# Sparse-attention indexer: three of eight heads summed on GpSimd, five on VectorE out of PSUM

## The chip, the cores and the metric

The kernel runs on one core of a Trainium2 chip. The metric is the device time of one execution in microseconds. The profile is of one execution, taken by the hardware profiler on the same core. The engines are TensorE (PE; PEld is its weight load), VectorE (DVE), ScalarE (ACT), GpSimd (POOL) and SyncE (SP, which issues DMAs).

## What is computed

Two layers of an encoder over 16 learned meta tokens and 1024 frames, width 1024. Layer 0 mixes tokens with chunked gated linear attention, layer 1 with sparse attention; a SwiGLU block follows each. The change lies in layer 1. Per block of 128 queries:

```python
s_idx = einsum('bqhd,bsd->bqhs', q_idx, k_idx) * IDX_DIM ** -0.5     # 8 indexer heads of 64
score = einsum('bqhs,bqh->bqs', relu(s_idx), w_idx)                  # weighted sum over heads
score = where(admissible, score, -inf)                               # chunk-causal
top_val, top_idx = top_k(score, 256)
logits = q_lat . c[top_idx] * ATT_HEAD_DIM ** -0.5 + rel_bias        # attention over the 256 keys
```

The kernel doesn't gather. It finds the 256th largest score of every query by bisection over the bits of the scores, writes a mask that is 0 for chosen keys and -1e30 elsewhere, and attends densely. Among equal scores the earlier keys win, as in `top_k`.

## The kernel before

Every f32 product is made of three passes over a high and a low part in fp32r (`mm3`, L223 to L227; `split`, L219 to L221, makes the parts: the high one on ScalarE, the low one on VectorE or on the engine named). All matmul results go through eight PSUM tiles of 512 columns (`ps`, L179). The program is written in one order; the compiler issues each engine's instructions in about that order and moves some ahead where they are ready. `Later` (L60) holds closures that fall due after a number of `tick` calls, one per unit of work.

Layer 1's mixer is `dsa` (L857). Its stages:

- **Keys and queries of the indexer** (L876 to L896). `kxh` and `kxl` hold the keys' parts, `wt` the head weights, which are turned into `wx`, one column per block and head. `index_queries` makes the queries' parts `qx`, in two ranges of frames and for two heads at a time.
- **Scores** (`score`, L898 to L915). A block b has 144 + 128 b keys, cut in pieces of at most 512 columns (one piece for blocks 1 and 2, two each for 3 to 6, three for 7; block 0 needs none). Per block, head and piece: two matmuls into PSUM, a Relu on ScalarE from PSUM into one of three `rt` buffers (L907), and on VectorE a multiply by the head's weight into `sc` (head 0, L910) or a multiply-add onto `sc` (L912). The early blocks 1 to 3 are interleaved with the second range of queries, two heads at a time; then the late blocks 4 to 7 follow, heads 0 to 7 of one block after the other. The `kx` and `relu` pools are closed behind it, and their space is used again by the masks and the top-k.
- **Top-k beside projections** (L937 to L982). A list of units (the latent `c`, L990 to L1031; the query projections, L1033 to L1055; `parts`, which splits the queries of heads 0 to 5 into `xh` and `xl`; keys and values of the first head pair) is issued in order, and steps of `topk` (L1057) are taken between them by a list of costs: 66 steps of bisection and 8 for masks. Blocks are in two groups. A step counts on ScalarE (L1090) and VectorE (L1093) how many scores lie above a candidate; `decide` (L1095) makes the next candidate on GpSimd (L1102 to L1106), in a fixed order, so it waits in GpSimd's queue behind whatever was issued there. Counting of the next step needs it.
- The latent units hold their results in PSUM until three of them are there; then VectorE scales them (L1018) and a closure, due 3 to 5 ticks later, transposes each on TensorE (`turn`, L1022, L1026) and splits it.
- `parts` handles three frame ranges, each in two groups j of three heads. For j = 1 (named in `QPOOL`) it splits head by head with GpSimd making the low parts, for j = 0 in one piece of 1032 columns with VectorE.
- **Masks** (L1189 to L1202). Per block: ScalarE takes the sign of threshold minus score (`sg`, and its sum), VectorE tests it for zero (L1196), makes a running count of the equal ones (`pre`, L1197), computes how many equal ones are still needed (L1198, L1199), and forms the mask (L1200, L1201).
- **Attention** (L1246): GpSimd adds the relative bias to the mask (L1263), then logits, softmax and mixing, pair by pair of blocks.

Weights that were split beforehand come by DMAs queued on GpSimd (`load_parts`, L195): the latent's at `w.ahead()` (L932), those of dq0 when the latent's are taken (L1001).

## Time and profile before

| | us |
|---|---|
| three runs | 2604.9, 2607.8, 2607.78 (median 2607.78) |
| the profiled execution | 2605.77 |
| its span in the profile | 2604.0 |
| mean granted clock of TensorE | 0.982 of full speed |

The page gives totals per engine, the span in 40 slices, DMA queues, the chain that ended last and the costliest groups. A busy TensorE there is not TensorE at its peak, since matmuls are pipelined; a row of a merged timeline gives its start, the time to the end of its last instruction, and how many. Layer 1's mixer runs from about 1285 to 1745 us of the span; the rows further down are from there.

### The profile page before, as it was taken

Reading aid. Unit: us, or ns where it says so; the run is one execution under the profiler, and the core shown is the slowest. Engines: PE = TensorE matmul, PEld = TensorE weight load, DVE = VectorE, ACT = ScalarE, POOL = GpSimd, SP = SyncE. Lnnn points to the kernel's source line nnn. Section 1 sums busy time; section 2 is a strip of 40 time slices with the busy share of each in tenths; the row PEclk is TensorE's granted clock in tenths of the full one; section 3 lists DMA queues with packets and bytes.
Section 4 is the critical chain, followed back from the end, with each engine's and each line's share of the span. In section 5 each row is a group of like instructions: output and inputs, shape, how many; then the busy total and the mean of one; then the engine's idle time right before and its main releaser. Section 6 shows DMA issues by size and latency. Waiting matters only on the chain.

```text
span 2604.0 us, 37955 instructions
## 1 busy us (share of the span) xinstructions
PE 2513.8 (97%) x15072; PEld 2333.6 (90%) x15072; DVE 1358.0 (52%) x2915; ACT 952.7 (37%) x1970; POOL 382.0 (15%) x582
## 2 busy tenths in 40 slices
PE   6999999999999999999898969999999999999997
PEld 6899999999999999999878959999988888888887
DVE  7565566643333333444679997762633333333336
ACT  5664453521111111112568867761511111111114
POOL 3000000111111111110203455440200000000001
PEclk9999999999999999999899969999999999999999
DMA  3103013123333333331311101122011111111111
GB/s 119 41 27 116 25 49 105 43 86 122 121 102 120 116 117 112 116 118 66 117 65 51 64 25 42 64 96 85 33 65 49 49 49 49 47 42 42 49 49 65
DMA packets 68788, 190.00 MB, mean 73 GB/s; under 512 B 7065, under 2 KB 18609, under 8 KB 65794
## 3 DMA queue, kind: packets, MB, share of 16 engines
q1 hardware_dynamic: 62642, 154.31, 17.6%
q0 software_dynamic: 5968, 33.26, 3.7%
q8 instruction: 118, 1.93, 0.3%
q14 instruction: 60, 0.49, 0.1%
HBM read 150.74 MB, written 41.58 MB: 74 GB/s over the span
## 4 chain that ended last, share of the span: by engine, by line
PE 41%; DVE 4%; issue 2%; ACT 2%; POOL 1%; DMA 0%; ACTq 0%; DVEq 0%; POOLq 0%
PE ps L226 13%; PE ps L227 13%; PE ps L225 13%; PE ps L1310 1%; DVE jd L1093 1%; POOL xl L221 1%; DVE sc L912 1%; PE ps L1322 1%; PE ps L903 0%; DVE pre L1197 0%; ACT ja L1090 0%; ACT rt L907 0%; PE ps L1298 0%; PE ps L905 0%; DVE h L332 0%
## 5 line engine op out<-in xcount | busy, mean ns | idle before, releaser
L225 PE MATMUL ps<-xh,wh 128*128 128x344 f32 (+6 forms) x2808 | 947.7, 338 | 5.8 <-ACT wh L191 4.1
L226 PE MATMUL ps<-xl,wh 128*128 128x344 f32 (+6 forms) x2808 | 943.9, 336 | 0.8 <-POOL xl L221 0.6
L227 PE MATMUL ps<-xh,wl 128*128 128x344 f32 (+6 forms) x2808 | 941.4, 335 | 3.0 <-DVE wl L192 3.0
L225 PEld LDWEIGHTS ps<-xh,wh 128*128 128x128 f32 x2808 | 530.3, 189 | 37.1 <-ACT wh L191 4.4
L226 PEld LDWEIGHTS ps<-xl,wh 128*128 128x128 f32 x2808 | 530.7, 189 | 30.2 <-POOL xl L221 1.4
L227 PEld LDWEIGHTS ps<-xh,wl 128*128 128x128 f32 x2808 | 530.3, 189 | 30.1 <-DVE wl L192 3.3
L703 DVE TENSOR_TENSOR t<-sg,ps 128x344 f32<-128x344 f32 (+4 forms) x116 | 65.1, 561 | 643.8 <-PE ps L227 643.0
L191 ACT CAST wh<-wraw 128x1056 fp32r<-128x1056 f32 (+2 forms) x160 | 163.9, 1049 | 582.4 <-PE ps L226 570.8
L716 DVE TENSOR_TENSOR h<-h,ps 128x344 f32<-128x344 f32 (+3 forms) x456 | 250.8, 566 | 163.6 <-PE ps L227 163.5
L225 PE MATMUL ps<-hh,wh 128*128 128x512 f32 (+2 forms) x800 | 280.3, 350 | 0.0
L226 PE MATMUL ps<-hl,wh 128*128 128x512 f32 (+2 forms) x800 | 280.0, 350 | 0.0
L227 PE MATMUL ps<-hh,wl 128*128 128x512 f32 (+2 forms) x800 | 279.8, 350 | 0.0
L192 DVE TENSOR_TENSOR wl<-wraw,wh 128x1056 fp32r<-128x1056 f32 (+2 forms) x158 | 195.1, 1257 | 73.8 <-ACT wh L191 72.9
L225 PE MATMUL ps<-wh,xh 128*128 128x256 f32 (+9 forms) x560 | 173.5, 310 | 11.5 <-ACT xh L220 7.4
L227 PE MATMUL ps<-wh,xl 128*128 128x256 f32 (+9 forms) x560 | 167.9, 300 | 4.1 <-POOL xl L221 2.1
L702 ACT ACTIVATE sg<-ps 128x344 f32<-128x344 f32 (+4 forms) x116 | 57.8, 498 | 303.5 <-PE ps L227 299.0
L226 PE MATMUL ps<-wl,xh 128*128 128x256 f32 (+9 forms) x560 | 166.8, 298 | 0.0
L220 ACT CAST hh<-t 128x344 fp32r<-128x344 f32 (+4 forms) x116 | 60.0, 517 | 285.3 <-DVE t L703 285.3
L225 PEld LDWEIGHTS ps<-hh,wh 128*128 128x128 f32 x800 | 150.1, 188 | 14.6
L226 PEld LDWEIGHTS ps<-hl,wh 128*128 128x128 f32 x800 | 150.3, 188 | 14.3
L227 PEld LDWEIGHTS ps<-hh,wl 128*128 128x128 f32 x800 | 150.5, 188 | 13.9
L225 PEld LDWEIGHTS ps<-wh,xh 128*128 128x128 f32 x560 | 109.6, 196 | 17.7 <-ACT xh L220 8.1
(286 smaller groups left out, 3378.6 us busy)
## 6 DMA issues: line engine op xcount, KB each, us to landing
wraw<-in_w_fi SPq DMA_DIRECT2D x44, 528.0 KB, 3.8
wraw<-in_w_fi SPq DMA_DIRECT2D x44, 496.0 KB, 4.9
wraw<-in_w_fo SPq DMA_DIRECT2D x22, 528.0 KB, 3.8
wraw<-in_w_fo SPq DMA_DIRECT2D x22, 496.0 KB, 5.1
s_skew<-s_rel POOLq DMA_DIRECT2D x8, 583.5 KB, 13.0
h<-in_ht SPq DMA_DIRECT2D x8, 520.0 KB, 5.8
wraw<-s_skew SPq DMA_DIRECT2D x8, 520.0 KB, 3.5
sg<-in_w_dq SPq DMA_DIRECT2D x16, 256.0 KB, 4.3
```

Source lines behind the costliest of these rows:

```text
L191: nc.scalar.copy(hi[:, a:e], r[:, : e - a])
L192: self.wlow.tensor_sub(lo[:, a:e], r[:, : e - a], hi[:, a:e].bitcast(F32))
L220: self.nc.scalar.copy(hi, src)
L221: (low or self.nc.vector).tensor_sub(lo, src, hi.bitcast(F32))
L225: mm(p, sh, mh, start=first, stop=False, skip_group_check=True)
L226: mm(p, sh, ml, start=False, stop=False, skip_group_check=True)
L227: mm(p, sl, mh, start=False, stop=last, skip_group_check=True)
L702: nc.scalar.activation(sg[:, :n], pg[:, :n], AF.Silu)
L703: v.tensor_mul(t[:, :n], sg[:, :n], pu[:, :n])
L716: v.tensor_add(self.h[:, d, a : a + n], self.h[:, d, a : a + n], p[:, :n])
L912: eng.scalar_tensor_tensor(o, rt, wx[:, b, hd : hd + 1], o, op0=OP.mult, op1=OP.add)
L1093: v.tensor_scalar(j[:, :n], mu(b), cand, None, op0=OP.is_lt, op1=OP.add, accum_out=out)
```

## The change

- `EARLY_HEADS = 3`: for heads 0 to 2 ScalarE's Relu still writes `rt` (four buffers now), but GpSimd does the sum: a multiply by the weight into `sc` for head 0, a multiply in place and an addition onto `sc` for heads 1 and 2. For heads 3 to 7 the Relu is written in place in PSUM and VectorE multiplies and adds from there onto `sc`.
- The late blocks are issued in another order: heads 0 to 2 of block 4, heads 0 to 2 of block 5, heads 3 to 7 of block 4, heads 0 to 2 of block 6, heads 3 to 7 of block 5, and so on; block 7's heads 3 to 7 come last. `w.ahead()` stands at the same place of the program.
- `QPOOL = (0, 1)`: the low parts of the queries of heads 0 to 5 are all made on GpSimd, head by head; their high parts are six casts per frame range where there were one wide and three.
- The transposes of the latent are due 5 to 7 ticks later instead of 3 to 5.
- Masks: the equality test is left out; ScalarE squares the sign, so that 0 marks an equal key, and the running count subtracts a tile of ones from it. The counts are negative now, and signs and the comparison in L1198 to L1200 turn accordingly. One memset of `ones` (1040 bf16 columns) is new.

```diff
+EARLY_HEADS = 3
-QPOOL, KEYS0, PC = (1,), 0, 1.0
+QPOOL, KEYS0, PC = (0, 1), 0, 1.0
...
-            with tc.tile_pool(name="kx", bufs=1) as kp, tc.tile_pool(name="relu", bufs=3) as rp:
+            with tc.tile_pool(name="kx", bufs=1) as kp, tc.tile_pool(name="relu", bufs=4) as rp:
...
                         nc.tensor.matmul(p, qx[:, hd, t], kxl[:, s0 : s0 + n], start=False, stop=True)
+                        o, wt = sc[:, off[b] + s0 : off[b] + s0 + n], wx[:, b, hd : hd + 1]
+                        if hd >= EARLY_HEADS:
+                            nc.scalar.activation(p, p, AF.Relu)
+                            v.scalar_tensor_tensor(o, p, wt, o, op0=OP.mult, op1=OP.add)
+                            continue
+
                         rt = rp.tile([128, 512], F32, name="rt")[:, :n]
                         nc.scalar.activation(rt, p, AF.Relu)
-                        o = sc[:, off[b] + s0 : off[b] + s0 + n]
                         if hd == 0:
-                            eng.tensor_scalar_mul(o, rt, wx[:, b, hd : hd + 1])
+                            nc.gpsimd.tensor_scalar_mul(o, rt, wt)
                         else:
-                            eng.scalar_tensor_tensor(o, rt, wx[:, b, hd : hd + 1], o,
-                                                     op0=OP.mult, op1=OP.add)
+                            nc.gpsimd.tensor_scalar_mul(rt, rt, wt)
+                            nc.gpsimd.tensor_add(o, o, rt)
...
-                w.ahead()
-                for b in range(4, 8):
-                    for hd in range(8):
-                        score(b, hd)
+                    if e == 3:
+                        w.ahead()
+
+                late = [[(b, hd) for hd in range(EARLY_HEADS, 8)] for b in range(4, 8)]
+                first = [[(b, hd) for hd in range(EARLY_HEADS)] for b in range(4, 8)] + [[]]
+                for b, hd in first[0] + sum((x + y for x, y in zip(first[1:], late)), []):
+                    score(b, hd)
...
-                self.later.at(3 + i % 3, lambda i=i, c=c: turn(i, c))
+                self.later.at(5 + i % 3, lambda i=i, c=c: turn(i, c))
...
+        ones = pool.tile([128, T], BF16, name="ones")
+        v.memset(ones, 1.0)
...
-            eq = mk(b)
+            other = mk(b)
...
-            v.tensor_scalar(eq, sg, 0.0, None, op0=OP.is_equal)
-            v.tensor_tensor_scan(pre, eq, eq, 0.0, op0=OP.add, op1=OP.bypass)
-            v.tensor_scalar(need, bal, 0.5, TOPK - n / 2, op0=OP.mult, op1=OP.add)
+            nc.scalar.activation(other, sg, AF.Square)
+
+            v.tensor_tensor_scan(pre, other, ones[:, :n], 0.0, op0=OP.add, op1=OP.subtract)
+            v.tensor_scalar(need, bal, -0.5, n / 2 - TOPK, op0=OP.mult, op1=OP.add)
             v.scalar_tensor_tensor(need, pre[:, n - 1 : n], 0.5, need, op0=OP.mult, op1=OP.add)
-            v.scalar_tensor_tensor(sg, pre, need, sg, op0=OP.is_le, op1=OP.subtract)
+            v.scalar_tensor_tensor(sg, pre, need, sg, op0=OP.is_ge, op1=OP.subtract)
```

## Rows read from the trace of the kernel before

**Rows 1.** The page's first part: busy time, share of the span, instructions of each engine.

```profile
PE 2513.8 (97%) x15072; PEld 2333.6 (90%) x15072; DVE 1358.0 (52%) x2915; ACT 952.7 (37%) x1970; POOL 382.0 (15%) x582
```

**Rows 2.** Busy time in five stretches (us; busy, instructions per engine; granted clock, DMA).

```profile
core 0: us, PE busy (x) PEld busy (x) DVE busy (x) ACT busy (x) POOL busy (x), PEclk, DMA share, GB/s
1336.80:1374.50 37.70, 37.53 (x171) 24.11 (x172) 37.67 (x82) 34.52 (x75) 0.00 (x0) 1.00 0.07 29
1374.50:1391.00 16.50, 9.06 (x78) 8.88 (x77) 13.44 (x68) 12.94 (x26) 3.31 (x11) 0.85 0.19 65
1391.00:1495.00 104.00, 104.00 (x679) 103.90 (x680) 102.15 (x271) 87.86 (x208) 48.97 (x210) 0.97 0.17 62
1495.00:1515.00 20.00, 9.06 (x49) 8.33 (x47) 17.39 (x45) 14.06 (x33) 14.48 (x39) 0.77 0.01 2
1515.00:1548.00 33.00, 20.76 (x83) 18.06 (x83) 32.94 (x77) 17.14 (x45) 11.68 (x11) 0.60 0.09 32
```

**Rows 3.** Timeline of the late scores, VectorE and ScalarE (start us, busy us, instructions merged).

```profile
1364.07 10.39 DVE L912 SCALAR_TENSOR_TENSOR sc<-rt,wx,sc 128x352 f32<-128x352 f32 x21
...
1336.76 35.82 ACT L907 ACTIVATE rt<-ps 128x264 f32<-128x264 f32 x72 [0.15 <-DVE sc L915]
```

**Rows 4.** Instructions that write xl, 1370 to 1560 us (duration ns min/median/max).

```profile
L221 POOL TENSOR_TENSOR xl<-qf,xh x9: 897/944/1946, 1495.9 to 1519.3; 128x344 fp32r<-128x344 f32 x6, 128x336 fp32r<-128x336 f32 x3
L1052 DVE SCALAR_TENSOR_TENSOR xl<-ps,xh x6: 498/506/511, 1492.5 to 1514.9; 128x344 fp32r<-128x344 f32 x4, 128x336 fp32r<-128x336 f32 x2
L221 DVE TENSOR_TENSOR xl<-qf,xh x3: 1200/1264/1852, 1497.5 to 1516.5; 128x1032 fp32r<-128x1032 f32 x2, 128x1008 fp32r<-128x1008 f32 x1
```

**Rows 5.** Waits, 1270 to 1400 us and 1391 to 1500 us (us in total, times, longest).

```profile
PE ps L1026 <- DVE qf L1018: 7.4, 1, 7.4
...
ACT qf L1043 <- PE ps L227: 2.8, 2, 2.1
```

**Rows 6.** Groups by shape, GpSimd, whole run (busy us, mean ns of one).

```profile
L213 POOL CAST eh<-sg 128x512 fp32r<-128x512 f32 x54 | 35.4, 656 | 526.1 <-DMA sg<-in_w_dq 156.1 <-DMA sg<-in_w_do 155.3 <-DMA sg<-in_w_qidx 92.3
L221 POOL TENSOR_TENSOR xl<-gkv,xh 128x256 fp32r<-128x256 f32 x32 | 23.6, 739 | 23.6 <-ACT xh L220 23.6
L1106 POOL TENSOR_SCALAR flip<-cand 128x4 f32<-128x4 f32 x29 | 6.7, 231 | 2.5
L360 POOL TENSOR_SCALAR w<-mean 96x128 fp32r<-96x128 f32 x4 | 2.0, 545 | 0.0
```

**Rows 7.** Timeline of GpSimd, 1332 us and 1495 to 1521 us (start us, busy us).

```profile
1332.51 0.53 POOL L200 DMA_DIRECT2D wh<-s_dq_h  x1 [14.60 <-PE ps L227]
...
1495.87 3.71 POOL L221 TENSOR_TENSOR xl<-qf,xh 128x344 fp32r<-128x344 f32 x3
...
1516.60 3.77 POOL L221 TENSOR_TENSOR xl<-qf,xh 128x336 fp32r<-128x336 f32 x3 [2.50 <-ACT xh L220]
```

**Rows 8.** Timeline of VectorE, 1382 us and 1500 to 1530 us (in brackets: idle before, releaser).

```profile
1382.26 0.12 DVE L1186 MEMSET mask<- 128x72 uint32 x1
...
1500.40 0.90 DVE L1093 TENSOR_SCALAR_CACHE_REDUCE jd<-mask,cand 128x656 bf16<-128x656 uint16 x1 [1.61 <-POOL cand L1104]
...
1517.63 0.86 DVE L1129 TENSOR_SCALAR y<-x 128x3 f32<-128x3 f32 x1
...
1527.56 0.32 DVE L1196 TENSOR_SCALAR mask<-sg 128x656 bf16<-128x656 bf16 x1
...
1527.89 1.26 DVE L1196 TENSOR_SCALAR mask<-sg 128x784 bf16<-128x784 bf16 x1
```

**Rows 9.** Groups by shape, ScalarE, whole run (busy us, mean ns of one).

```profile
L1090 ACT ACTIVATE ja<-mask,cand 128x1040 bf16<-128x1040 uint16 x31 | 36.0, 1161 | 7.8 <-POOL cand L1104 6.5 <-DVE mask L1168 0.7
...
L1090 ACT ACTIVATE ja<-mask,cand 128x272 bf16<-128x272 uint16 x31 | 15.8, 509 | 0.0
```

**Rows 10.** DMA issues, 1300 to 1500 us (KB each, median us to landing).

```profile
wh<-s_dq_h POOLq DMA_DIRECT2D x4, 1024.0 KB, 5.4
```

**Rows 11.** Instructions that read wh, 1375 to 1420 us (first and last start).

```profile
L225 PEld LDWEIGHTS ps<-xh,wh x29: 187/188/191, 1405.8 to 1419.6; 128*128 128x128 f32 x29
```

More of the change, by code (lines that the diff above doesn't have):

```diff
@@ L871, in dsa @@
             sc = dp.tile([128, off[8]], F32, name="sc")
-            with tc.tile_pool(name="kx", bufs=1) as kp, tc.tile_pool(name="relu", bufs=3) as rp:
+            with tc.tile_pool(name="kx", bufs=1) as kp, tc.tile_pool(name="relu", bufs=4) as rp:
                 kxh = kp.tile([128, T], F32R, name="kxh")
                 kxl = kp.tile([128, T], F32R, name="kxl")
-                wt = kp.tile([128, T], F32, name="wt")
+                hw = kp.tile([128, T], F32, name="wt")
                 for a, n in ALL:
@@ L880, in dsa @@
                         nc.scalar.copy(kxh[r : r + 64, s], p[0:64, :n])
-                    nc.scalar.copy(wt[64:128, s], p[64:128, :n])
+                    nc.scalar.copy(hw[64:128, s], p[64:128, :n])
                     for r in (0, 64):
@@ L899, in score @@
                     t = slice((b - 1) * 128, b * 128)
-                    eng = v
                     for s0, n in cut(nkeys(b)):
@@ L922, in dsa @@
                             a = META + 128 * b
-                            nc.tensor.transpose(p[:, b * 64 : b * 64 + 64], wt[64:128, a : a + 128],
+                            nc.tensor.transpose(p[:, b * 64 : b * 64 + 64], hw[64:128, a : a + 128],
                                                 self.ident[64:128, 64:128])
```

## The prediction, made before the changed kernel was run

> **What bounds the kernel now.** I read the page's totals first: TensorE is busy for 97% of the span [rows 1], so a change to the other engines can only act where TensorE idles or is paced. Then busy time by stretch [rows 2], which finds that place, the indexer and its top-k. In 1336.8 to 1374.5 (scores of blocks 4 to 7) VectorE has 37.67 of 37.70 us in use and GpSimd does nothing. In 1391 to 1495 (bisection beside the query projections) VectorE has 102.15 of 104 us, in 1515 to 1548 (masks) 32.94 of 33. TensorE's matmul rows also fill 1391 to 1495, but it idles for 7.4 us before that, for 10.9 us in 1495 to 1515 and 12.2 us in 1515 to 1548. TensorE therefore has slack, and VectorE's queue sets when attention starts: what delays or shortens it moves the end nearly one for one.
>
> Third, the timeline of the late scores [rows 3]. ScalarE issues 72 Relus in 35.82 us, 0.50 us apart. The last 21 VectorE sums take 10.39 us, also 0.495 us each, and end at 1374.5. Relu follows sum because only three rt buffers stand between them. Until 1374.5 no bisection starts. Last, the waits [rows 5]: the 7.4 us of TensorE before 1391 is one wait, L1026 (transposes of the latent) for VectorE's L1018; ScalarE twice waits for a query projection, 2.8 us in all.
>
> **The change, part by part.** I sum against the profiled execution (2605.8 us, span 2604.0); it lies 2.0 us under the median of the three runs, and I take nothing for that.
>
> *Scores, VectorE and ScalarE.* Of 104 VectorE sums 39 go, 27 of them late (9 key pieces x 3 heads). The 45 late ones that remain read PSUM instead of rt. The nearest row that reads PSUM, L1052, takes 0.506 us at 344 columns [rows 4], so I keep 0.495 us: 45 x 0.495 = 22.3 us. VectorE gets slack. ScalarE keeps its Relus, now 45 of the 72 in place; if it can't go faster than 0.50 us apart it ends at 1372.6, so the gain here is at most about 2 us. In-place tiles hold their PSUM bank until VectorE has read; with 8 banks I charge nothing.
>
> *Scores, GpSimd.* Late, three heads need 27 multiplies and 18 additions, of 391 columns on average (3520 columns per head in 9 pieces). An addition: GpSimd's subtraction of two f32 tiles takes 0.944 us at 344 columns [rows 4] and 0.739 at 256 [rows 6], so 1.05 us at 391; 18 x 1.05 = 19.0 us. For a multiply no row has this width. Its own kind, TENSOR_SCALAR, takes 0.231 us at 4 columns and 0.545 at 128 [rows 6]. Drawn on in a straight line (2.53 ns a column) that makes 0.545 + 263 x 0.00253 = 1.21 us; with the steepest slope that the CAST row allows (0.656 us / 512 = 1.28 ns) 0.88 us; and if the multiply were a CAST altogether, 0.656 x 391 / 512 = 0.50 us. The row nearest in kind is TENSOR_SCALAR, so I take the middle of the first two, 1.05 us: 28.4 us (23.8 to 32.7; as a CAST 13.5). GpSimd's late work is then 47.4 us (42.8 to 51.7; 32.5).
>
> GpSimd can't begin it before the first late Relu at 1336.8, since the early blocks' pieces come first in the program. It ends at 1384.2. Block 7 comes last in the new order, and VectorE's five heads add onto GpSimd's three: behind GpSimd's last piece stand 5 sums (2.5 us, if the heads of a piece go together) to 13 (6.4 us, in the order written). The trace has Relus issued between casts that the program lists first, so order bends to readiness: 2.5 us, end 1386.7. Against 1374.5 that is **+12.2 us** (1382.1 to 1394.9: +7.6 to +20.4). The fourth rt buffer lets ScalarE run one piece further ahead and doesn't make GpSimd faster.
>
> The dq0 load queued on GpSimd moves behind this work: issued at 1332.5 [rows 7], it would go at 1384. It lands 5.4 us later [rows 10], and its first use, 1405.8 [rows 11], moves back too, so nothing.
>
> *Latent transposes two units later.* More projection work stands ahead of L1026, so its 7.4 us of idle TensorE is filled. That pays only where VectorE or ScalarE waits for TensorE later: the 2.8 us [rows 5]. I take **-1** (-2.8 to 0).
>
> *Low parts of queries.* Three VectorE subtractions go, 1.2 to 1.85 us each [rows 4], and GpSimd gets nine more in three bunches; the old bunches take 3.71 and 3.77 us, first and last of three [rows 7]. Behind the first two stand the decisions (L1102 to L1106), on which the next counts on VectorE and ScalarE wait. In the first, VectorE already idles 1.61 us for a decision [rows 8] after its own subtraction, so removing that frees nothing; three more ahead of a decision cost up to 3.7 us. Two places at 0 to 3.7: I take half, +3.7. The third bunch meets the mask code. There a TENSOR_SCALAR of 3 columns, L1129, takes 0.86 us on VectorE [rows 8] beside GpSimd's subtractions, some 0.7 more than its size explains; three more subtractions, 3 x 0.7 = 2.1, less the freed 1.2, give +0.9. Sum **+4.6** (-1.2 to +8.3).
>
> The Trainium skill (SBUF — State Buffer, Who interferes with whom) says that such VectorE instructions and GpSimd share a port pair that one of them holds for its whole instruction. The trace agrees in kind (0.86 us). Held for three whole subtractions, VectorE would lose 3.7 instead of 2.1 us, and the sum would be 1.6 us higher.
>
> *Masks.* Seven is_equal tests leave VectorE: 0.32 us at 656 columns, but 1.26 at 784, beside a GpSimd addition [rows 8]: 7 x 0.32 + 0.9 = 3.1 us. If the hold merely passes to the next instruction, 2.2. A memset of ones comes: 72 words take 0.12 us [rows 8], 520 words up to 0.87; I take 0.4. Seven squares come to ScalarE, 0.51 to 1.16 us by the bisection's rows at 272 and 1040 columns [rows 9]; ScalarE is busy for 17.14 of 33 us there [rows 2] and two sg buffers let it run ahead, so only the first, 0.5 us, is exposed. Bound: VectorE waits for a square once per pair of blocks, 4 x 0.84 = 3.4. The scan has the same width and I leave its price. The other sum's low end takes ones and the first square at nothing (-3.1). Sum -3.1 + 0.4 + 0.2 = **-2.5** (-3.1 to +1.6), the first square half covered by a query cast.
>
> 12.2 - 1 + 4.6 - 2.5 = +13.3: 2605.8 + 13.3 = 2619.1, **2619 us**.
>
> **Rivals.** *GpSimd multiplies cheaply, faster.* For: its CAST, one input like the multiply, takes 0.656 us for 512 columns. Against: TENSOR_SCALAR takes nearly that for 128. At 0.50 us the late work ends at 1336.8 + 32.5 = 1369.3 and VectorE's tail at 1371.8, with ScalarE's end at 1372.6: -2. With fast GpSimd the decisions aren't late (-1.2), transposes -1, masks -3.1: 2605.8 - 7.3 = 2598.5 us. Its point is where GpSimd's work is 35.2 us, a multiply of (35.2 - 19.0) / 27 = 0.60 us; below it the score stage shortens. The Trainium skill (GPSIMD Engine Reference, 4.1 Engine selection) calls one-input work on GpSimd roughly line-rate, which speaks for this rival; no row here shows it for TENSOR_SCALAR. Chance 0.22.
>
> *Costs and savings cancel, no change.* Multiply at the lower slope (+7.6), decisions find gaps (-1.2), transposes pay in full (-2.8), masks -2.7: +0.9, 2606.7 us. For: VectorE's new idle time can take other blocks' sign counts, and the compiler may move late multiplies forward into GpSimd's earlier gap. Chance 0.20.
>
> *The forecast, a late GpSimd.* 0.58. Own range 2610 to 2632; all upper bounds together would be +30.3, 2636.
>
> **How the numbers follow.** A measurement of this kernel can tell about 0.2%, 5.2 us, from no change: 2602.6 to 2613.0. The three cases fall faster, same, slower: 0.22, 0.20, 0.58. The range runs from 2597, which takes in most of the cheap rival, to 2632.
>
> **What would show it.** GpSimd nearly full from 1337 to about 1384, multiplies near 1.05 us, VectorE with idle time released by GpSimd in the scores, and the first sign count (L1136, now at 1375) 10 us later. Decisions behind six subtractions, with VectorE idle 3 to 5 us twice. No is_equal on VectorE, and TensorE's wait at L1026 gone. Multiplies at or under 0.6 us, or a first sign count by 1373, would make it wrong, as would attention starting on time in spite of late scores.

## The result, and the profile after

| | before | after |
|---|---|---|
| median | 2607.79 us (2604.9 to 2608.03, 4 runs) | 2635.44 us (2634.08 to 2637.3, 4 runs) |
| profiled execution, span | 2605.77, 2604.0 | 2634.08, 2632.3 |

The changed kernel is slower, ratio 1.011 with a 95% interval of 1.0095 to 1.0125: 27.7 us, where the forecast said 13 and its range ended at 2632. The sign and the place were right, the size was off by a factor of two. Of the runs further down, one execution of e10 took 13901 us and is left out of its median.

To see where the time went, four points are marked in both traces: ScalarE's first wide cast of queries, VectorE's first sign count (start of the bisection), the cast of the last decision for the first group of blocks (the four with 128x4; the other group's follows 1.8 us later in both kernels), and the first 128x128 transposes of the attention. First the timelines of the kernel before at these points.

```profile
1309.00 0.58 ACT L895 CAST qx<-ps 64x512 fp32r<-64x512 f32 x1 [3.08 <-PE ps L227]
...
1375.07 1.23 DVE L1136 TENSOR_SCALAR_CACHE_REDUCE jd<-sc 128x1040 bf16<-128x1040 uint16 x1
...
1513.73 0.17 DVE L1155 CAST th<-cand 128x4 uint16<-128x4 f32 x1
...
1548.26 0.90 PE L1310 MATMUL ps<-ident,sc 128*128 128x128 f32 x3 [1.51 <-DVE mask L1202]
```

The same four points after:

```profile
1307.07 0.58 ACT L896 CAST qx<-ps 64x512 fp32r<-64x512 f32 x1 [3.08 <-PE ps L228]
...
1398.08 1.23 DVE L1144 TENSOR_SCALAR_CACHE_REDUCE jd<-sc 128x1040 bf16<-128x1040 uint16 x1
...
1540.59 0.17 DVE L1163 CAST th<-cand 128x4 uint16<-128x4 f32 x1
...
1576.16 0.90 PE L1321 MATMUL ps<-ident,sc 128*128 128x128 f32 x3 [1.61 <-DVE sm L1289]
```

The differences give three stretches, used from here on: **scores** 66.07 us before and 91.01 after (+24.9), **bisection** 138.66 and 142.51 (+3.9), **masks** 34.53 and 35.57 (+1.0). The first point itself lies anywhere from 1307 to 1312 us in the runs, whatever the kernel.

Busy time after, which answers to [rows 1]:

```profile
PE 2519.2 (96%) x15072; PEld 2342.3 (89%) x15072; DVE 1341.8 (51%) x2867; ACT 954.6 (36%) x1983; POOL 455.2 (17%) x656
```

Two stretches, the early blocks and the late scores; the second answers to the first of [rows 2]:

```profile
core 0: us, PE busy (x) PEld busy (x) DVE busy (x) ACT busy (x) POOL busy (x), PEclk, DMA share, GB/s
1307.00:1341.20 34.20, 30.47 (x143) 24.38 (x141) 13.38 (x25) 16.00 (x42) 20.73 (x24) 0.95 0.27 92
1341.20:1397.50 56.30, 43.12 (x168) 34.83 (x168) 25.90 (x56) 30.73 (x73) 50.79 (x47) 0.76 0.08 27
```

VectorE's total fell by 16.2 us against [rows 1] and GpSimd's rose by 73.2. In the late scores VectorE now works 25.90 of 56.30 us and GpSimd 50.79: the bound seems to have passed to GpSimd, which e3 tests. TensorE, which had work in 37.53 of 37.70 us there before, idles 13 of 56; its granted clock is 0.76 in the mean there, between its two levels of 1.2 and 2.4 GHz, and was 1.00. The timeline of GpSimd (start, busy, instructions merged):

```profile
1308.11 0.98 POOL L915 TENSOR_SCALAR sc<-rt,wx 128x272 f32<-128x272 f32 x1 [21.49 <-ACT rt L913]
...
1325.93 1.43 POOL L918 TENSOR_TENSOR sc<-sc,rt 128x264 f32<-128x264 f32 x2
...
1341.40 2.19 POOL L915 TENSOR_SCALAR sc<-rt,wx 128x328 f32<-128x328 f32 x2 [3.27 <-ACT rt L913]
1343.58 2.18 POOL L917 TENSOR_SCALAR rt<-rt,wx 128x328 f32<-128x328 f32 x2
1345.73 1.70 POOL L918 TENSOR_TENSOR sc<-sc,rt 128x328 f32<-128x328 f32 x2
...
1353.75 2.50 POOL L917 TENSOR_SCALAR rt<-rt,wx 128x392 f32<-128x392 f32 x2
1356.22 2.00 POOL L918 TENSOR_TENSOR sc<-sc,rt 128x392 f32<-128x392 f32 x2
...
1389.23 1.80 POOL L918 TENSOR_TENSOR sc<-sc,rt 128x352 f32<-128x352 f32 x2
```

Two blocks of work without gaps: the early blocks' sums from 1308.1 to 1327.4, and the late ones from 1341.40 to 1391.03, which is 49.6 us. A multiply (TENSOR_SCALAR) of 392 columns takes 1.25 us, an addition 1.00. VectorE's timeline shows who waits:

```profile
1323.15 0.50 DVE L909 SCALAR_TENSOR_TENSOR sc<-ps,wx,sc 128x272 f32<-128x272 f32 x1 [5.00 <-POOL sc L918]
...
1350.47 0.56 DVE L909 SCALAR_TENSOR_TENSOR sc<-ps,wx,sc 128x328 f32<-128x328 f32 x1 [7.34 <-POOL sc L918]
...
1384.02 6.58 DVE L909 SCALAR_TENSOR_TENSOR sc<-ps,wx,sc 128x456 f32<-128x456 f32 x11 [11.87 <-ACT ps L908]
...
1390.60 6.87 DVE L909 SCALAR_TENSOR_TENSOR sc<-ps,wx,sc 128x352 f32<-128x352 f32 x14
```

Behind GpSimd's end at 1391.03 stand 13 sums, until 1397.47 (one of the 14 in the last row starts before it). The wait of 11.87 us ends with a Relu on ScalarE, not with GpSimd. ScalarE's Relus into rt wait 21.3 us in this stretch for GpSimd's sums, which free the buffers; e3 asks whether four buffers are the bound. In the early blocks head 3's sum waits for GpSimd (5.00 us). The next query parts stand behind it in VectorE's queue, and the second cast of the third pair of heads, on ScalarE, waits for them:

```profile
1328.64 0.58 ACT L896 CAST qx<-ps 64x512 fp32r<-64x512 f32 x1 [4.37 <-DVE qx L897]
```

### The profile page after: what moved, and what is told of

Same layout as the page of the kernel before. It is cut to its first block, busy times and chain, and to the rows that moved or that the text cites. A ratio compares the mean times of both kernels' runs of the same rounds, so it can differ in the third digit from the quotient of the medians.

```text
span 2632.3 us, 37984 instructions
## 1 busy us (share of the span) xinstructions
PE 2519.2 (96%) x15072; PEld 2342.3 (89%) x15072; DVE 1341.8 (51%) x2867; ACT 954.6 (36%) x1983; POOL 455.2 (17%) x656
## 4 chain that ended last, share of the span: by engine, by line
PE 42%; DVE 3%; POOL 3%; issue 1%; ACT 1%; DMA 0%; ACTq 0%; DVEq 0%; POOLq 0%
PE ps L227 13%; PE ps L228 13%; PE ps L226 13%; PE ps L1321 1%; POOL rt L917 1%; POOL sc L918 1%; POOL xl L222 1%; POOL sc L915 1%; PE ps L1333 1%; DVE pre L1208 0%; DVE jd L1101 0%; PE ps L1309 0%; DVE h L333 0%; DVE sg L1211 0%; ACT L321 0%
## 5 line engine op out<-in xcount | busy, mean ns | idle before, releaser
L227 PEld LDWEIGHTS ps<-xl,wh 128*128 128x128 f32 x2808 | 531.4, 189 | 30.4 <-POOL xl L222 1.4
L294 POOL TENSOR_TENSOR nb<-nb,nq 128x256 f32<-128x256 f32 x12 | 9.1, 758 | 711.7 <-ACT nq L292 711.7
```

The costliest lines, as they stand in the source:

```text
L227: mm(p, sh, ml, start=False, stop=False, skip_group_check=True)
```

## The experiments

Every run was timed beside the kernel before on the same chip, whose medians were 2605.85 (e1 to e4), 2605.53 (e5, e6, e7, e10), 2605.81 (e8, e9, e11, e12) and 2604.48 us (e13 to e16). Differences in the text are between medians; the ratio is worked out from the runs together and differs from that of the medians by up to 0.04%. The last three columns are the stretches of one profiled execution, read off as above. In the ten kernels, the one before among them, whose low parts and transposes are unchanged, the bisection took 138.56 to 139.26 us, so differences under 0.7 us in that column say nothing.

| run | median us | ratio, 95% interval | scores | bisection | masks |
|---|---|---|---|---|---|
| e1 scores only | 2631.97 | 1.0097 [1.0081, 1.0114] | 90.90 | 139.22 | 34.53 |
| e2 rest only | 2609.75 | 1.0016 [1.0007, 1.0026] | 66.07 | 142.93 | 35.55 |
| e3 eight rt buffers | 2635.63 | 1.0114 [1.0099, 1.0129] | 90.95 | 142.44 | 35.55 |
| e4 early on VectorE | 2629.15 | 1.0089 [1.0074, 1.0104] | 85.90 | 140.83 | 35.55 |
| e5 tail by piece | 2635.72 | 1.0118 [1.0103, 1.0133] | 91.29 | 142.27 | 35.55 |
| e14 block 7 by piece | 2632.13 | 1.0106 [1.0093, 1.0120] | 88.20 | 142.24 | 35.55 |
| e10 no head (nine executions) | 2607.38 | 1.0010 [1.0000, 1.0020] | 68.72 | 138.80 | 34.22 |
| e6 one head | 2604.05 | 0.9996 [0.9986, 1.0005] | 64.56 | 138.95 | 34.24 |
| e7 two heads | 2609.76 | 1.0014 [1.0005, 1.0023] | 70.27 | 139.26 | 34.53 |
| e11 one head, early rt | 2604.07 | 0.9993 [0.9984, 1.0002] | 64.41 | 138.73 | 34.23 |
| e12 three heads, early rt | 2627.07 | 1.0080 [1.0064, 1.0095] | 85.86 | 138.68 | 34.22 |
| e8 low parts only | 2609.06 | 1.0010 [1.0001, 1.0019] | 66.06 | 141.32 | 36.07 |
| e9 masks only | 2603.96 | 0.9995 [0.9987, 1.0004] | 66.06 | 138.56 | 33.59 |
| e13 transposes only | 2606.23 | 1.0008 [0.9999, 1.0017] | 66.08 | 139.60 | 34.53 |
| e15 one head, from block 5 | 2603.29 | 0.9993 [0.9984, 1.0002] | 64.13 | 139.14 | 33.61 |
| e16 two heads, from block 5 | 2599.44 | 0.9980 [0.9971, 0.9989] | 61.83 | 138.61 | 33.61 |

### Which part: e1 and e2

e1 is the kernel before with the score stage alone, e2 the changed kernel with the old score stage.

Against the changed kernel, e1 takes back these lines and the mask section, e2 everything from the `kx` and `relu` pools to the late blocks' order:

```diff
-QPOOL, KEYS0, PC = (0, 1), 0, 1.0
+QPOOL, KEYS0, PC = (1,), 0, 1.0
...
-                self.later.at(5 + i % 3, lambda i=i, c=c: turn(i, c))
+                self.later.at(3 + i % 3, lambda i=i, c=c: turn(i, c))
```

> The kernel before with the new score stage alone (heads split between GpSimd and VectorE, new order, four rt buffers). My theory: the score stage carries nearly all of the 27.6 us. Its end moves from 1374.5 to 1397.5 in the trace, so this kernel should take 2607.8 + 23 = 2631 us (2628 to 2633), with GpSimd full from 1341 to 1391. Rival: the queries' low parts and the masks carry half of it; then this kernel takes under 2622.

> The changed kernel with the old score stage: low parts on GpSimd, later transposes and the masks by a square remain. My theory: bisection +3.9 and masks +1.0 us by the stretches of the two traces, so 2612.7 us (2610 to 2615). Rival (the savings that the change means to make are real and the late scores only hide them): 2600 to 2606, faster than before.

26.1 us and 3.9 us: the score stage carries the loss, as the first theory has it, and its rival falls. The rest costs a little less than expected, but it costs. Together that is 30.0 us, where the result has 27.7; e3, which has both parts and was timed beside the same runs of the kernel before, is 29.8 us slower.

### What sets the end of the scores: e3, e4, e5, e14

e3 is the changed kernel with eight rt buffers, e4 the changed kernel with the early blocks' sums on VectorE:

```diff
-... tc.tile_pool(name="relu", bufs=4) as rp:
+... tc.tile_pool(name="relu", bufs=8) as rp:
```

```diff
-                        if hd >= EARLY_HEADS:
+                        if hd >= EARLY_HEADS or b < 4:
                             nc.scalar.activation(p, p, AF.Relu)
-                            v.scalar_tensor_tensor(o, p, wt, o, op0=OP.mult, op1=OP.add)
+                            if hd:
+                                v.scalar_tensor_tensor(o, p, wt, o, op0=OP.mult, op1=OP.add)
+                            else:
+                                v.tensor_scalar_mul(o, p, wt)
                             continue
```

> The changed kernel with eight rt buffers in place of four, so that ScalarE's Relus for VectorE's heads stand less behind GpSimd. My theory: GpSimd's own 49.6 us of late work and the 13 sums of VectorE behind its last piece set the end, so the late stretch stays; only the early stretch, where ScalarE's casts of queries wait behind rt, gives back 1 to 3 us: 2632 to 2635. Rival (the ring of rt buffers is the bound, since 25 sums of VectorE follow ScalarE's last rt Relu at 1383): the tail shrinks by 10 or more sums of 0.54 us, so 2630 or less.

> The changed kernel, but in the early blocks 1 to 3 VectorE sums all eight heads out of PSUM; GpSimd sums three heads of the late blocks only. My theory: the early GpSimd sums (19.2 us) hold VectorE's and ScalarE's query parts behind them and start the late blocks 6 us late; without them the late blocks start 6 us earlier and the rest follows, 2635.4 - 6 = 2629.4 us (2628 to 2631.5). Rival (the late blocks wait for something else, the early sums are hidden beside TensorE's query projections as I had reckoned): 2634 to 2637.

Eight buffers give back nothing, not even the 1 to 3 us that the theory gave them in the early blocks. ScalarE's Relus had seemed to come too late, but with more buffers VectorE's last row still waits for GpSimd and then has the same 13 sums to do:

```profile
1395.10 6.40 DVE L909 SCALAR_TENSOR_TENSOR sc<-ps,wx,sc 128x336 f32<-128x336 f32 x13 [0.27 <-POOL sc L918]
```

So the four buffers are not the bound, and GpSimd's work is. e4 comes out as expected: with the early blocks' sums back on VectorE the scores take 85.90 us instead of 91.01. The early sums on GpSimd cost 5.1 us; e1 and e12 below, without the rest of the change, differ by 5.0.

e5 and e14 ask for the price of the 13 sums. e5 (with eight buffers) issues only VectorE's five heads of block 7 by pieces, e14 also GpSimd's three.

The third argument of `score` is the only piece to do; e5 has the second of the two loops, e14 both:

```diff
+                for s0, n in cut(nkeys(7)):
+                    for _, hd in first[3]:
+                        score(7, hd, s0)
                 for b, hd in late[2]:
                     score(b, hd)
+                for s0, n in cut(nkeys(7)):
+                    for _, hd in late[3]:
+                        score(7, hd, s0)
```

> The changed kernel with eight rt buffers, and block 7's heads 3 to 7 issued piece by piece (all five heads of one piece, then of the next) instead of head by head. Theory: 13 VectorE sums (6.4 us) stand behind GpSimd's last addition because the written order has four heads of three pieces behind head 3's first; by pieces only 5 remain (2.5 us), so the bisection starts 3.9 us earlier and the kernel takes about 2631.5 us (2630 to 2633). Rival: ScalarE's Relus or TensorE's products set the end as well, so that a shorter tail only moves the wait: 2634 to 2637.

> The changed kernel with eight rt buffers and all of block 7 issued piece by piece: GpSimd's three heads of one piece, then of the next, and VectorE's five heads likewise at the end. In the earlier run only VectorE's part was by pieces, GpSimd finished all three pieces within its last 6 us, and 13 sums still stood behind its end. Theory: now the first two pieces are whole 4 to 8 us before GpSimd's end, 5 sums (2.5 us) stand behind it, and the kernel takes 2631 to 2633 us, 3 to 4 us less than the changed kernel. Rival: VectorE's or TensorE's order keeps a tail of 10 sums or more: 2634 to 2637.

e5 missed its theory and changed nothing, and it doesn't decide: GpSimd, still head by head, finished block 7's three pieces within its last 4 us, and VectorE's last 13 sums begin with a wait for the last but one of its additions. GpSimd's end is 1394.98:

```profile
1394.17 4.98 DVE L911 SCALAR_TENSOR_TENSOR sc<-ps,wx,sc 128x352 f32<-128x352 f32 x10 [1.86 <-POOL sc L920]
```

In e14 the two orders agree. GpSimd's last row, and VectorE's rows around it:

```profile
1393.16 1.88 POOL L920 TENSOR_TENSOR sc<-sc,rt 128x336 f32<-128x336 f32 x2
```

```profile
1391.01 3.53 DVE L911 SCALAR_TENSOR_TENSOR sc<-ps,wx,sc 128x352 f32<-128x352 f32 x7 [2.14 <-POOL sc L920]
1395.07 1.53 DVE L911 SCALAR_TENSOR_TENSOR sc<-ps,wx,sc 128x336 f32<-128x336 f32 x3 [0.52 <-POOL sc L920]
```

The seven sums of the first row start ahead of GpSimd's end (1395.04), the last at 1394.0, and six are left behind it. The scores take 88.20 us instead of 90.95 in e3 and 91.29 in e5: the order of the tail is worth some 3 us. The whole times alone would not show it: the intervals of e14, e3 and e5 overlap.

### How the loss grows with the heads: e10, e6, e7, e11, e12

These are the kernel before with the score stage alone, and EARLY_HEADS at 0, 1 and 2. Early blocks are summed on VectorE, out of PSUM in e10, e6 and e7, from rt in e11 (EARLY_HEADS at 1) and e12 (at 3).

e10, e6 and e7 have e4's lines and another number, as e6 here:

```diff
-EARLY_HEADS = 3
+EARLY_HEADS = 1
```

e11 (with that number) and e12 (with 3) have these:

```diff
-                        if hd >= EARLY_HEADS:
+                        if hd >= EARLY_HEADS and b >= 4:
...
-                            nc.gpsimd.tensor_scalar_mul(o, rt, wt)
+                            (v if b < 4 else nc.gpsimd).tensor_scalar_mul(o, rt, wt)
+                        elif b < 4:
+                            v.scalar_tensor_tensor(o, rt, wt, o, op0=OP.mult, op1=OP.add)
```

> As the one-head kernel, with no head on GpSimd: every Relu in place in PSUM, every sum on VectorE out of PSUM. It asks what reading PSUM alone does. Theory: a sum from PSUM takes what one from rt takes (0.49 to 0.50 us), VectorE stays full: no change, 2604.5 to 2607.5 us. Rival: the three rt buffers held the two engines in step, and PSUM frees them: 2 to 5 us faster; or a read from PSUM is dearer, 72 x 0.05 us: 3 to 4 us slower.

> The kernel before with one change: head 0 of the late blocks is multiplied on GpSimd, everything else is summed on VectorE out of PSUM, early blocks altogether on VectorE; low parts, transposes and masks as before. Theory: nine multiplies of 1.24 us are 11.2 us on GpSimd, far from a bound; VectorE's late work falls from 72 to 63 sums (31.2 us for 35.7), and ScalarE, which needed 30.7 us for its 72 Relus in the changed kernel, can follow: 3 to 5 us faster than before, 2601 to 2603 us. Rival: the 0.50 us between Relus is ScalarE's or TensorE's own pace, so nothing is gained: 2605 to 2608.

> As the one-head kernel, with heads 0 and 1 of the late blocks on GpSimd. Theory: 18 multiplies of 1.24 us and 9 additions of 0.99 us make GpSimd's late work 31.2 us; with VectorE's last sums behind it (some 16 of 0.49 us in the written order) the stage is 38 to 39 us against 37.7 before: 2606 to 2609 us. That is about 16 us less than the three-head kernel with the same early blocks (some 2625 us by the earlier runs). Rival: the cost is in the handover between the engines and not in GpSimd's sum of durations, so that two heads cost nearly what three do: 2615 or more.

> As the one-head kernel (2604.05 us), but the early blocks' Relus go to rt again, as in the kernel before. Theory: in-place Relus hold their PSUM tiles until VectorE's sums have read them, so that the next query product waits for a tile; the stretch from the first wide query cast to the first sign count was 68.7 us without any head on GpSimd against 66.1 before, though the late part was no longer. With rt in the early blocks those 2 to 3 us come back: 2600.5 to 2602.5 us, faster than the kernel before by 3 to 5 us. Rival: the 2.7 us have another cause (order of issue): 2603.5 to 2605.

> The changed kernel's late scores alone (three heads on GpSimd, five out of PSUM), early blocks as in the kernel before, low parts, transposes and masks as before. Theory: GpSimd's late work of 49.6 us starts where the kernel before starts its late scores, some 28 us behind the first wide query cast, and 13 sums follow: 28 + 49.6 + 6.4 = 84 us for 66.1, less a little for the first Relus: 16 to 18 us slower than before, 2621.5 to 2624 us. Rival: the early blocks' form doesn't matter for GpSimd's start: 2625 to 2627 as the earlier run with early sums on VectorE, less the rest's 3.9 us.

Scores of 68.7, 64.6, 70.3 and 85.9 us for 0, 1, 2 and 3 heads: the first head helps by 4.2, the second costs 5.7, the third 15.6 more. (The three-head kernel is e12, whose early blocks read rt; between e6 and e11 that form makes 0.15 us.) The third head adds nine multiplies and nine additions, 9 x (1.22 + 0.98) = 19.8 us of GpSimd's time, of which 15.6 show. At two heads GpSimd is done 10 us before VectorE, and still it costs, since each block's first sums wait for it, directly or through ScalarE, whose in-place Relus stand behind Relus that wait for an rt buffer. VectorE in e7, then ScalarE's wait there (in total, times, longest):

```profile
1342.06 0.56 DVE L910 SCALAR_TENSOR_TENSOR sc<-ps,wx,sc 128x328 f32<-128x328 f32 x1 [3.57 <-POOL sc L921]
...
1350.88 0.63 DVE L910 SCALAR_TENSOR_TENSOR sc<-ps,wx,sc 128x392 f32<-128x392 f32 x1 [2.76 <-ACT ps L908]
...
1360.98 0.69 DVE L910 SCALAR_TENSOR_TENSOR sc<-ps,wx,sc 128x456 f32<-128x456 f32 x1 [3.56 <-ACT ps L908]
```

```profile
ACT rt L916 <- POOL sc L921: 4.3, 6, 1.1
```

Before the first sums of blocks 4, 5 and 6 VectorE idles 3.57, 2.76 and 3.56 us. The time (+4.2 us) is 0.8 us above the expected range, far from its rival.

One head missed it: 1.5 us faster and not to be told from no change, where 3 to 5 were expected. e10 has the reason. The late multiply-adds cost the same (14 of 392 columns in 7.62 us from rt, 7.55 from PSUM), but head 0's multiply, which it moves from rt to PSUM, was the cheap one. In the kernel before, and then in e10:

```profile
1345.99 0.35 DVE L910 TENSOR_SCALAR sc<-rt,wx 128x392 f32<-128x392 f32 x1
```

```profile
1347.39 0.55 DVE L912 TENSOR_SCALAR sc<-ps,wx 128x392 f32<-128x392 f32 x1
```

Taking head 0 from VectorE saves nine times 0.32 to 0.45 us, not nine times 0.5. The other part of e10's extra 2.7 us of scores lies in the early blocks: the pairs of wide casts follow each other 8.3 us apart, in e11 7.8. TensorE's waits in e10 from 1307 to 1334 us point to the in-place Relus, whose PSUM tiles stay taken until VectorE has read them:

```profile
PEld ps L226 <- DVE sc L910: 0.5, 2, 0.2
PEld ps L903 <- DVE sc L910: 0.3, 2, 0.2
```

With two more rows of 0.2 us these are 1.2 us; the kernel before and e11 have no such wait in that stretch. No run varies the number of PSUM tiles. e11 got the 0.5 us per pair back and yet stayed at e6's time, by its rival: VectorE's first two late sums out of PSUM wait there for GpSimd's multiplies, 0.83 and 0.53 us, and the second starts 31.5 us behind the wide cast, where e6 starts the first at 31.0 without a wait.

e12 also came out by its rival, at its upper end: 2627.07 where 2621.5 to 2624 was expected. GpSimd starts 28.9 us behind the cast, works 49.9, and 6.4 of sums and 0.6 of small work follow: 85.9, as in e4, where it starts 29.3 us behind. The early blocks' form hardly matters to GpSimd's start.

### The rest, part by part: e8, e9, e13

Each is the kernel before with one edit of the change: e8 this one, e9 the mask section, e13 the line of `turn`.

```diff
-QPOOL, KEYS0, PC = (1,), 0, 1.0
+QPOOL, KEYS0, PC = (0, 1), 0, 1.0
```

> The kernel before with one change: all low parts of heads 0 to 5's queries on GpSimd, head by head. Theory: of the 3.9 us that the changed kernel's rest (low parts, transposes, masks) cost together, the low parts are the cause, since decisions stand behind six subtractions in GpSimd's queue: 3 to 5 us slower than before, 2608.5 to 2611 us, and the stretch from first sign count to the last decision's cast 3 to 5 us longer. Rival: the later transposes did it, and the low parts are worth nothing: 2605 to 2607.

> The kernel before with one change: the equality test by a square on ScalarE, with the tile of ones. Theory: the mask stage, which was 1.0 us longer in the changed kernel, was longer for GpSimd's subtractions beside it; alone the masks save 1 to 2.5 us of VectorE's time: 2603 to 2605 us. Rival: the square and its handover cost what the test did, also alone: 2605 to 2607.5.

> The kernel before with one change: the latent's transposes due 5 to 7 ticks later instead of 3 to 5. Low parts alone cost 3.3 us and masks alone saved 1.9, together 1.4; the whole rest cost 3.9. Theory: the later transposes cost the other 2.5 us: 2607.5 to 2609.5 us. Rival 1: they are worth nothing alone (2605 to 2607) and low parts and masks cost more together than alone, since GpSimd's subtractions lie beside the mask code. Rival 2, as predicted: about 1 us faster, 2604 to 2605.

Low parts cost 3.3 us. The masks gain 1.9 by an interval that takes in no change; their stretch is 0.9 shorter. The transposes cost 1.8, by an interval that takes in no change too: the time lies in the first rival's range (worth nothing alone), the difference at the theory's lower end, and the bisection is 0.9 longer. Neither is clear of noise by its time alone. Their sum is 3.2 against e2's 3.9: the parts add up, within the intervals. In e8, GpSimd's first bunch:

```profile
1494.00 5.36 POOL L221 TENSOR_TENSOR xl<-qf,xh 128x344 fp32r<-128x344 f32 x6
```

VectorE's next count behind it:

```profile
1500.17 0.90 DVE L1093 TENSOR_SCALAR_CACHE_REDUCE jd<-mask,cand 128x656 bf16<-128x656 uint16 x1 [4.43 <-POOL cand L1104]
```

The idle time for a decision is 4.43 us where it was 1.61 [rows 8]; 1.26 of the difference is VectorE's own subtraction, which is gone. Six subtractions took 5.36 us where three had taken 3.71, so the decision itself comes 1.65 us later, not up to 3.7. In the second bunch a decision stands between the third subtraction and the fourth, and VectorE idles twice more, 1.62 us where it did not before and 2.00 where it was 0.83:

```profile
1510.49 0.63 DVE L1093 TENSOR_SCALAR_CACHE_REDUCE jd<-mask,cand 128x400 bf16<-128x400 uint16 x1 [1.62 <-POOL cand L1104]
...
1514.22 0.16 DVE L1153 TENSOR_TENSOR cand<-cand,sgn 128x4 f32<-128x4 f32 x1 [2.00 <-POOL cand L1104]
```

e13's waits (in total, times, longest), in the bisection:

```profile
ACT qf L1043 <- PE ps L227: 6.6, 3, 4.5
...
PE ps L1026 <- DVE qf L1018: 4.2, 2, 2.4
```

TensorE's wait for the latent falls from 7.4 to 4.2 us, and ScalarE's for the query projection rises from 2.8 to 6.6 [rows 5].

### A version that beats both: e15 and e16

Block 4 is summed wholly on VectorE, its first head (e15) or two (e16) from rt and the others, unlike in the kernel before, out of PSUM, and its 16 sums cover GpSimd's first pieces of block 5. The early blocks are summed on VectorE from rt. From block 5 on GpSimd has one head (e15), or two with eight rt buffers (e16). Both have the new masks and none of the other parts.

```diff
-EARLY_HEADS = 3
+EARLY_HEADS = 2
...
-                        if hd >= EARLY_HEADS:
+                        if hd >= EARLY_HEADS and b >= 4:
...
-                            nc.gpsimd.tensor_scalar_mul(o, rt, wt)
+                            (v if b < 5 else nc.gpsimd).tensor_scalar_mul(o, rt, wt)
+                        elif b < 5:
+                            v.scalar_tensor_tensor(o, rt, wt, o, op0=OP.mult, op1=OP.add)
...
+                late[0], first[0] = first[0] + late[0], []
```

These are e16's lines against the changed kernel, beside eight rt buffers and the old low parts and transposes; e15 has EARLY_HEADS at 1 and four buffers.

> Scores with head 0 of blocks 5 to 7 on GpSimd, blocks 1 to 4 as in the kernel before, the other late sums out of PSUM, and the changed kernel's masks. Theory: with block 4 on VectorE nothing waits for GpSimd's first multiplies, 7 of VectorE's 72 sums go (3.5 us), and the masks save 1.9 us: 5 us faster than before, 2600 to 2602 us. Rival: VectorE's sums beside GpSimd's get dearer or ScalarE's Relus hold them, so that 1 to 2 us remain with the masks': 2602.5 to 2604.5.

> As the last, with heads 0 and 1 of blocks 5 to 7 on GpSimd and eight rt buffers. Theory (the amount and the place of GpSimd's work decide): 14 multiplies and 7 additions are 24.5 us on GpSimd, spread under some 30.4 us of VectorE's 58 sums, none of which waits: 14 fewer sums are 6.9 us, ScalarE's 72 Relus at 31 to 32.5 us take 1 to 2 of it back, masks save 1.9: 2597 to 2600 us. Rival: handing sums over costs waits at every block, as in the two-head kernel that was 4 us slower than before: 2605 or more.

e15 came out by its rival, 1.2 us under the kernel before and not to be told from it: seven cheap multiplies are worth little. e16 came out by its theory: it gained 5.0 us, with an interval of 0.1 to 0.3%, and beats the kernel before and the changed one. VectorE at e16's handovers, then GpSimd's last row:

```profile
1346.51 0.63 DVE L909 SCALAR_TENSOR_TENSOR sc<-ps,wx,sc 128x392 f32<-128x392 f32 x1 [0.38 <-ACT ps L908]
...
1353.84 0.69 DVE L909 SCALAR_TENSOR_TENSOR sc<-ps,wx,sc 128x456 f32<-128x456 f32 x1 [0.79 <-POOL sc L915]
```

```profile
1361.28 0.91 POOL L920 TENSOR_TENSOR sc<-sc,rt 128x336 f32<-128x336 f32 x1
```

The idle time per block is 0.38 and 0.79 us, where e7 had 2.76 and 3.56. GpSimd stops at 1362.2, VectorE at 1370.1: nothing but VectorE's own sums is left behind it. Scores are 4.2 us shorter, masks 0.9. Against e7, e16 differs in four things at once: block 4 on VectorE, so that GpSimd works 25.5 us and not 30.4, eight rt buffers, early blocks from rt, and the masks. That eight buffers alone would have cured e7, by its waits for them, is a rival that no run tests.

## Why the prediction was right in sign and wrong in size

**GpSimd as the new bound: right.** Late work without gaps, VectorE idle behind it, the first sign count late, as written, though it came 24.9 us later and not 10. e3 shows that the rt buffers, and the Relus held by them, don't set the end. The cheap-multiply rival fell: it needed 0.60 us or less, and the multiply took 1.22 in the mean. The second rival, costs and savings that cancel, fell with it. The dq0 load didn't move behind the late work: it went out at 1337.07, ahead of it, which cost nothing either way.

**The size failed in the sum of the score stage**, +12.2 forecast and +24.9 measured. Four terms make up the difference:

- *The early blocks were left out.* The step said that GpSimd can't begin its late work before 1336.8, and priced only the late pieces. The 12 multiplies and 8 additions of blocks 1 to 3, which the diff moves to GpSimd too, were never costed. They fill 1308 to 1327 and delay the queries through VectorE's queue: **+5.1 us** (e4). The second rival even counts on "GpSimd's earlier gap", which is where they stand.
- *The tail was taken at its low end.* Of the bounds 2.5 and 6.4 us the forecast took 2.5, since order had been seen to bend to readiness. The written order held: 13 sums, 6.4 us, **+3.9**. e14 got some 3 of it back, so this one was for the kernel to choose.
- *The multiply was taken in the middle.* 27 multiplies at 1.05 us; the groups of the trace give 32.9 us, 1.22 each. The additions were 0.98, not 1.05. Together they span 49.6 us for 47.4: **+2.2**. The width was wrong as well: blocks 4 to 7 have 656, 784, 912 and 1040 keys, 3392 in all and 377 a piece, not 3520 and 391. At 377 columns the same working gives 1.02 us for the multiply, 1.17 as its upper bound, and 45.9 us in all, so the multiply was further off than 2.2 us tell, and above its bound; the row that came nearest was its own kind drawn on in a straight line (1.21 us at 392 columns, where the trace has 1.256).
- *The start* was **1.1** us later than 1336.8 even without early sums, 28.9 us behind the cast for 27.8 (e12).

5.1 + 3.9 + 2.2 + 1.1 = 12.3, which with the forecast's 12.2 makes 24.5 of 24.9 us. Of the 16.3 us between 2619.1 and the median, another 2.0 were in the base: the sum went by the profiled execution of the kernel before, which lay that far under its median, and took nothing for it.

**Low parts: right in the main**, +4.6 forecast, +3.3 measured (e8), by decisions behind GpSimd's subtractions, and a third bunch against the masks (+1.5 us there, 0.9 forecast). One decision stood behind six of them, not two; the other bunch was split by a decision, and VectorE idled 1.62 and 2.00 us there, not 3 to 5. In the changed kernel VectorE idled 4.36 us at the first:

```profile
1526.11 0.90 DVE L1101 TENSOR_SCALAR_CACHE_REDUCE jd<-mask,cand 128x656 bf16<-128x656 uint16 x1 [4.36 <-POOL cand L1112]
```

behind this row of GpSimd:

```profile
1520.01 5.28 POOL L222 TENSOR_TENSOR xl<-qf,xh 128x344 fp32r<-128x344 f32 x6
```

**Transposes: wrong in sign as far as it can be told**, -1 forecast and +1.8 measured, with an interval from just under no change to 0.17%. TensorE's wait was taken for a loss to be filled, with ScalarE's 2.8 us of waiting as the gain. The wait at L1026 is not gone but 4.2 us, and ScalarE's wait for the query projection rose to 6.6; that the work pushed ahead of the transposes makes the projection late fits these rows and is argued.

**Masks: right in sign as far as it can be told**, -2.5 forecast, -1.9 measured alone (e9), of which the trace shows 0.9 in the stretch. The seven equality tests, 3.9 us, went as forecast, but the sum left the running count's price (10.7 us, then 11.7) and put the memset of ones at 0.4 us, which took 0.93; slow rows beside GpSimd's work passed to other instructions (L1199's seven took 1.0 us before and 2.5 in e9), which the forecast had as a bound. In the changed kernel the masks' stretch is 1.0 us longer all the same, where the low parts alone make it 1.5 us longer (e8) and the masks alone 0.9 shorter (e9).

The chances were right to put slower first. The range ended 3.4 us short: the early sums had no bound at all, and all upper bounds together, 2636 by the forecast's own sum, were cut to 2632. A range to 2636 would have held the time, but by luck, without the early sums in it.

## What to carry to other kernels

When work moves to another engine, list every instruction that the diff moves, the early ones under other work too, and follow what they hold up in the queues of the other engines. Work for a slow engine pays best where the fast engine has enough of its own meanwhile, and only until its sum reaches that stretch: the third head cost 15.6 us here, and two heads of three blocks, with more buffers, took 4.2 off the scores. Which of the two did it is not separated. Look for what the moved instructions cost where they were: head 0's multiplies were the cheapest of VectorE's sums.

## What was not expected of the hardware

- GpSimd's multiply of one f32 tile by a per-partition scalar is dearer than its addition of two tiles. Groups by shape of the changed kernel:

```profile
L917 POOL TENSOR_SCALAR rt<-rt,wx 128x456 f32<-128x456 f32 x4 | 5.6, 1415 | 0.0
L917 POOL TENSOR_SCALAR rt<-rt,wx 128x392 f32<-128x392 f32 x4 | 5.0, 1256 | 0.0
...
L918 POOL TENSOR_TENSOR sc<-sc,rt 128x456 f32<-128x456 f32 x4 | 4.5, 1147 | 0.0
...
L918 POOL TENSOR_TENSOR sc<-sc,rt 128x392 f32<-128x392 f32 x4 | 4.0, 1009 | 0.0
```

  (1415 - 1256) / 64 = 2.5 ns a column, against 656 ns / 512 = 1.28 ns for a CAST by [rows 6]. The Trainium skill (GPSIMD Engine Reference, 4.1 Engine selection) calls one-input work there roughly line-rate. The multiply's rows differ, and they decide: here the price of one such operation did not hold for another.
- Of the three subtractions on GpSimd that took 3.71 us together [rows 7], two took 0.93 and 0.94 us, and the one that ran beside VectorE's subtraction of two SBUF tiles took 1.95. The two in the kernel before:

```profile
1497.63 1.95 POOL L221 TENSOR_TENSOR xl<-qf,xh 128x344 fp32r<-128x344 f32 x1
```

```profile
1497.52 1.26 DVE L221 TENSOR_TENSOR xl<-qf,xh 128x1032 fp32r<-128x1032 f32 x1
```

  In the changed kernel, where VectorE's is gone, each of the six of that bunch took 0.90 to 0.92 us. The engine that keeps its work can get faster by what leaves the other. The Trainium skill (SBUF — State Buffer, Who interferes with whom) has a VectorE instruction with two SBUF inputs contend with a GpSimd instruction that reads there; these rows agree.
- On VectorE a multiply by a scalar took 0.35 us from SBUF and 0.55 from PSUM at 392 columns, while 14 multiply-adds took 7.62 and 7.55 us.
